# Down product of two FFNs as 2x2 block products of column chunk pairs, with seven products in some k-tile pairs

## Chip, cores and metric

The kernel runs on one core of a Trainium2 chip. The metric is device time in microseconds, the median of several executions; one further execution was recorded by the hardware profiler, and all rows below come from it.

## The reference

One decoder layer on 256 tokens of width 2048 in float32: half an FFN, a token mixer (two head groups of attention that read one input projection), another half FFN. The change touches the two FFNs (d_ff is 5632) and, at its edges, what stands next to them:

```python
def swiglu(x, w_gate, w_up, w_down):
    return (jax.nn.silu(x @ w_gate) * (x @ w_up)) @ w_down

x = x + 0.5 * swiglu(rms_norm(x, ffn1_norm[l]), ffn1_w_gate[l], ffn1_w_up[l], ffn1_w_down[l])
h = rms_norm(x, mix_norm[l])
parts = jnp.split(h @ w_in[l], split_at, axis=-1)
...
x = x + y @ w_out[l]
x = x + 0.5 * swiglu(rms_norm(x, ffn2_norm[l]), ffn2_w_gate[l], ffn2_w_up[l], ffn2_w_down[l])
```

## The kernel before

Tokens are two tiles of 128 (t = 0, 1), contraction goes in k-tiles of 128, columns in chunks of 512. Every product is made of three matmuls: both operands are split into a rounded high part and the rest (`split`, L195: a ScalarE cast to fp32r, a VectorE subtraction), and high x high, low x high and high x low are summed in one PSUM bank. Weights stream from memory into `w_raw` (three buffers), and are split into `w_hi` and `w_lo` (two buffers each).

An FFN goes over its 11 column chunks in parts of 4, 4 and 3 (`FF_PARTS`). For the first chunk gate and up are made as two plain products (`plain_pair`, `linear`); for every other chunk `pair` makes them together. A pair of k-tiles, the two token tiles and the two weight chunks (gate, up) form a 2x2 by 2x2 block product, eight products of three matmuls each. At the k-tile pairs j = 1, 3, 5 of eight (`STRASSEN`) it is made with seven products of sums instead: sums of activation blocks (S1 to S4, NS3) and sums of weight blocks (`w_t`, split into `t_hi`, `t_lo`, one buffer each). At the other j four of the eight products use differences (S3, DD) so that the results fall into the same PSUM sums. These are m2, m4, m5, m3 in the four main banks and m1, m6, m7 in three side banks; the fourth side bank serves all transposes meanwhile (`misc`). Behind the last seven step s1, v and u are formed, at the end seven more VectorE operations and two SiLUs make the chunk's result `g`. Then main and side banks swap (`banks.swap`).

The activation sums of x are made once for an FFN (`put_sums`, from a scaled copy `xf`). A chunk's result is transposed on TensorE in two halves of four transposes (`to_gT`, L358) and split into `ghi` and `glo` by one cast and one subtraction a half. After each part the down product runs over four column chunks, one after the other, with the plain `linear` (L217 on): per k-tile six matmuls, no sums, all four side banks free for transposes. Its result is added to the residual `xr` by two VectorE operations a chunk (L487). In the last part each finished chunk of `xr` goes on at once: in FFN 1 it is normalised for the mixer (`Stage.chunk`: transposes, splits, squares), in FFN 2 it is sent out (`to_out`).

Background work is written as generators (`spawn`); `pump` gives each one step after every six matmuls, and `wait(n)` lets n steps pass. The program order on each engine is set by a scheduler that lays instructions out by modelled times. `fpool` holds the temporaries of an FFN; in FFN 1 it closes in the last part behind the first down chunk (`to_mixer`), and the pool of the mixer's temporaries opens behind FFN 1.

## Time and profile before

| | us |
|---|---|
| median of 3 runs | 1868.89 (1868.73 to 1869.9) |
| profiled execution | 1867.15 |
| its span, first to last instruction | 1865.4 |
| TensorE busy | 1851.4 (99%) |
| VectorE busy | 1307.1 (70%) |
| ScalarE busy | 895.9 (48%) |
| granted TensorE clock, mean | 0.999 |

The three parts of FFN 1 lie at 5 to 729 us, the mixer at 729 to 1150, FFN 2 at 1150 to 1861. Within an FFN stretches of pairs and stretches of down follow each other. Matmuls overlap, so the busy time of one (about 0.39 us) is not what it takes; the distance between starts is.

### The profile page before, as it was taken

The numbers are of one execution on the slowest core, as the hardware profiler recorded it, in microseconds if no ns is written. First come the engines' busy times: TensorE is split into PE (matmuls) and PEld (weight loads), VectorE is DVE, ScalarE is ACT, GpSimd is POOL, SyncE is SP. The second block draws the span as 40 slices with busy tenths as digits, with TensorE's granted clock in tenths as the row PEclk, the third lists the DMA queues.
The fourth block names the chain that finished last, engine by engine and source line by source line (L and its number), as shares of the span: only waits on it lengthen the run. The fifth ranks groups of instructions, "written<-read, shape, count | busy, mean of one in ns | idle before, by whom it ended". The sixth has DMA issues, their size and how long they took to land.

```text
span 1865.4 us, 21669 instructions
## 1 busy us (share of the span) xinstructions
PE 1851.4 (99%) x8624; PEld 1528.4 (82%) x8626; DVE 1307.1 (70%) x1334; ACT 895.9 (48%) x904; POOL 4.8 (0%) x23
## 2 busy tenths in 40 slices
PE   9999999999999999999999999999999999999999
PEld 7778888888888888788888888888888887888887
DVE  6888568887478865656655567788647887558864
ACT  7545435454345445345455555454434554335542
POOL 0000000000000000000000000000000000000000
PEclk9999999999999999999999999999999999999999
DMA  8655555565566556764533445656556555556654
GB/s 298 208 190 186 194 190 202 194 202 191 189 216 203 195 200 203 237 219 147 155 128 113 144 161 192 203 182 201 198 187 208 198 195 188 192 191 204 203 195 143
DMA packets 190565, 356.60 MB, mean 191 GB/s; under 512 B 9312, under 2 KB 26624, under 8 KB 190464
## 3 DMA queue, kind: packets, MB, share of 16 engines
q1 hardware_dynamic: 188720, 354.65, 57.1%
q8 instruction: 67, 1.10, 0.2%
q10 hardware_dynamic: 1744, 0.58, 0.1%
q14 instruction: 34, 0.28, 0.0%
HBM read 353.09 MB, written 2.10 MB: 190 GB/s over the span
## 4 chain that ended last, share of the span: by engine, by line
PE 97%; ACT 1%; DVE 1%; issue 1%; DMA 0%; SPq 0%; ACTq 0%
PE m L449 15%; PE m L451 15%; PE m L450 15%; PE down L258 9%; PE down L259 9%; PE down L260 9%; PE in L260 4%; PE in L258 4%; PE in L259 4%; PE wo L258 1%; PE wo L259 1%; PE wo L260 1%; PE gt L366 1%; PE no L866 1%; PE gate L258 1%; PE gate L259 1%
## 5 line engine op out<-in xcount | busy, mean ns | idle before, releaser
L197 DVE TENSOR_TENSOR w_lo<-w_raw,w_hi 128x2048 fp32r<-128x2048 f32 (+3 forms) x331 | 709.1, 2148 | 365.0 <-ACT w_hi L196 364.5
L196 ACT CAST w_hi<-w_raw 128x2048 fp32r<-128x2048 f32 (+3 forms) x331 | 591.2, 1798 | 628.8 <-PE down L259 242.0
L449 PE MATMUL m<-w_hi,xhi 128*128 128x512 f32 x980 | 384.0, 392 | 2.2 <-ACT w_hi L196 1.9
L450 PE MATMUL m<-w_hi,xlo 128*128 128x512 f32 x980 | 381.9, 390 | 0.0
L451 PE MATMUL m<-w_lo,xhi 128*128 128x512 f32 x980 | 320.1, 390 | 0.8 <-DVE w_lo L197 0.8
L259 PE MATMUL down<-w_hi,glo 128*128 128x512 f32 x704 | 274.3, 390 | 0.0
L258 PE MATMUL down<-w_hi,ghi 128*128 128x512 f32 x704 | 273.2, 390 | 0.0
L260 PE MATMUL down<-w_lo,ghi 128*128 128x512 f32 x704 | 260.9, 390 | 0.0
L449 PEld LDWEIGHTS m<-w_hi,xhi 128*128 128x128 f32 x980 | 184.0, 188 | 43.5 <-ACT w_hi L196 5.3
L451 PEld LDWEIGHTS m<-w_lo,xhi 128*128 128x128 f32 x980 | 183.9, 188 | 41.2 <-DVE w_lo L197 2.9
L450 PEld LDWEIGHTS m<-w_hi,xlo 128*128 128x128 f32 x980 | 184.0, 188 | 37.7
L197 DVE TENSOR_TENSOR t_lo<-w_t,t_hi 128x2048 fp32r<-128x2048 f32 x60 | 137.3, 2288 | 47.2 <-ACT t_hi L196 47.2
L196 ACT CAST t_hi<-w_t 128x2048 fp32r<-128x2048 f32 x60 | 114.6, 1910 | 103.6 <-DVE w_t L435 101.3
L258 PEld LDWEIGHTS down<-w_hi,ghi 128*128 128x128 f32 x704 | 132.2, 188 | 27.3
L259 PEld LDWEIGHTS down<-w_hi,glo 128*128 128x128 f32 x704 | 132.2, 188 | 27.1
L260 PEld LDWEIGHTS down<-w_lo,ghi 128*128 128x128 f32 x704 | 131.9, 188 | 27.1
L258 PE MATMUL in<-w_hi,xhi 128*128 128x512 f32 (+3 forms) x384 | 146.1, 381 | 0.0
L259 PE MATMUL in<-w_hi,xlo 128*128 128x512 f32 (+3 forms) x384 | 143.8, 375 | 0.0
L260 PE MATMUL in<-w_lo,xhi 128*128 128x512 f32 (+3 forms) x384 | 141.2, 379 | 1.0 <-DVE w_lo L197 0.9
L449 PE MATMUL m<-t_hi,xhi 128*128 128x512 f32 x240 | 94.5, 397 | 1.8 <-ACT t_hi L196 1.8
L432 DVE TENSOR_TENSOR w_t<-w_raw 128x1024 f32<-128x1024 f32 x60 | 73.2, 1221 | 29.1 <-DMA w_raw<-in_ffn_w_gate 28.5
L450 PE MATMUL m<-t_hi,xlo 128*128 128x512 f32 x240 | 92.9, 390 | 0.0
(248 smaller groups left out, 1795.2 us busy)
## 6 DMA issues: line engine op xcount, KB each, us to landing
w_raw<-in_ffn_w_down SPq DMA_DIRECT2D x88, 1024.0 KB, 5.0
w_raw<-in_ffn_w_gate SPq DMA_DIRECT2D x163, 512.0 KB, 4.7
w_raw<-in_ffn_w_up SPq DMA_DIRECT2D x160, 512.0 KB, 3.8
w_raw<-in_w_in SPq DMA_DIRECT2D x36, 1024.0 KB, 5.0
w_raw<-in_w_out SPq DMA_DIRECT2D x16, 1024.0 KB, 4.9
w_raw<-in_ffn_w_up SPq DMA_DIRECT2D x8, 1024.0 KB, 5.4
w_raw<-in_ffn_w_gate SPq DMA_DIRECT2D x6, 1024.0 KB, 5.1
w<-in_cmp_k_w SPq DMA_DIRECT2D x8, 512.0 KB, 6.4
```

The costliest lines, as they stand in the source:

```text
L196: cast = nc.scalar.copy(hi, src)
L197: nc.vector.tensor_tensor(lo, src, hi.bitcast(F32), op=ALU.subtract)
L258: nc.tensor.matmul(po[t][:, :n], xhi, whi[:, j], start=s, stop=False)
L259: nc.tensor.matmul(po[t][:, :n], xlo, whi[:, j], start=False, stop=False)
L260: nc.tensor.matmul(po[t][:, :n], xhi, wlo[:, j], start=False, stop=e)
L366: nc.tensor.transpose(pt[:, j * SEQ + t * P:j * SEQ + (t + 1) * P], sg[t][:, (2 * i + j) * P:(2 * i + j + 1) * P], ident)
L432: nc.vector.tensor_tensor(ts[:, 0:2], raw[:, 0:1].to_broadcast([P, 2, CH]), raw[:, 1:4:2], op=ALU.subtract)
L449: nc.tensor.matmul(pm[m], ahi, bhi, start=first, stop=False)
L450: nc.tensor.matmul(pm[m], alo, bhi, start=False, stop=False)
L451: nc.tensor.matmul(pm[m], ahi, blo, start=False, stop=end)
L866: nc.tensor.matmul(po[:, h * HD:(h + 1) * HD], pT[:kn, h * P:(h + 1) * P], vv, start=first and h == 0, stop=True, skip_group_check=True)
```

## The change

`blocks` is `pair`'s loop made general: the weights' loads, the source of the activation forms, the seven steps and an action behind the last of them (`middle`) are arguments. `pair` calls it as before. `down` calls it for two column chunks at a time (0 and 1, then 2 and 3), with the 2x2 blocks of `g` in place of x and the two chunks of w_down in place of gate and up. Seven steps are those of j = 1, 3, 5 that are below nj - 1: three of eight pairs in the parts of four chunks, two of six in the last part. `middle` adds s1, v and u to the residual behind the last seven step; five more additions follow at the end. `to_gT` makes the sums of `g` once per part, for each half from a copy `gf` of the transposes. In the last part the residual chunks are handed on in the middle of the end additions and behind them. Around it: the pools are divided, so that `fpool` with the weight sums stays open until FFN 1's end (`fxpool` holds the forms of x); `xf` shares the buffers of `w_t` and `t_lo`; s1, v, `gf` and the rotary angles share one buffer; the sums of x start 8 instead of 14 pumps behind a load; squares go to PSUM; the two masks become one, read with a zero stride; the start-up zeros use a weight buffer.

```diff
-    idle = spool.tile([P, CH], BF16, tag="sq", bufs=1, name="idle")
+    idle = wpool.tile([P, CH], BF16, tag="wlo", name="idle")
...
-            self.pool = None
+            self.pool = self.tmp = None
         def square(self, c):
             for t in range(NT):
-                sq = spool.tile([P, CH], F32, tag="sq", bufs=1, name="sq")
-                nc.scalar.activation(sq, xr[t][c], AF.Square, accum_out=self.ssq[:, t, c:c + 1])
+                nc.scalar.activation(misc("sq"), xr[t][c], AF.Square, accum_out=self.ssq[:, t, c:c + 1])
...
             yield from wait(later)
             n = self.width(gi)
-            xf = self.pool.tile([P, 8, P], F32, tag="xf", bufs=2, name="xf")
+            xf = self.tmp.tile([P, 8, P], F32, tag=("ts", "tlo")[gi % 2], name="xf")
...
     def ffn(st, wg, wu, wd, after, fpool, last_part, groups=None):
-        ghi, glo = {}, {}
+        g = {}
...
-        def to_gT(slot, sg):
+        wdv = wd.rearrange("(k p) n -> p k n", p=P)
+        def to_gT(slot, sg, odd):
             yield from wait(2)
-            hi = gpool.tile([P, 4, SEQ], F32R, tag=f"ghi{slot}", name="ghi")
-            lo = gpool.tile([P, 4, SEQ], F32R, tag=f"glo{slot}", name="glo")
+            hi = gpool.tile([P, 8, P], F32R, tag=f"ghi{slot}", name="ghi")
+            lo = gpool.tile([P, 8, P], F32R, tag=f"glo{slot}", name="glo")
+            xhi = fpool.tile([P, 5, P], F32R, tag=f"gxhi{slot}", name="gxhi")
+            xlo = fpool.tile([P, 5, P], F32R, tag=f"gxlo{slot}", name="gxlo")
+            def put(x, o, n, src):
+                h, l = ((hi, lo), (xhi, xlo))[x]
+                split(h[:, o:o + n], l[:, o:o + n], src)
+            def where(x, o):
+                h, l = ((hi, lo), (xhi, xlo))[x]
+                return h[:, o], l[:, o]
             for i in range(2):
-                pt = misc("gt")
-                for j in range(2):
-                    for t in range(NT):
-                        nc.tensor.transpose(pt[:, j * SEQ + t * P:j * SEQ + (t + 1) * P],
-                                            sg[t][:, (2 * i + j) * P:(2 * i + j + 1) * P], ident)
-                split(hi[:, 2 * i:2 * i + 2].rearrange("p a b -> p (a b)"),
-                      lo[:, 2 * i:2 * i + 2].rearrange("p a b -> p (a b)"), pt)
+                seven = i == 1 and odd
+                pt = misc("gt").rearrange("p (a b) -> p a b", b=P)
+                order = ((0, 1), (0, 0), (1, 0), (1, 1)) if seven else ((0, 0), (0, 1), (1, 0), (1, 1))
+                for n, (j, t) in enumerate(order):
+                    nc.tensor.transpose(pt[:, n], sg[t][:, (2 * i + j) * P:(2 * i + j + 1) * P], ident)
+                gf = fpool.tile([P, 8, P], F32, tag="sv", name="gf")
+                nc.scalar.copy(gf[:, :4], pt)
+                if seven:
+                    put(1, 0, 3, pt[:, 1:])
+                    nc.vector.tensor_tensor(gf[:, 4], gf[:, 0], gf[:, 1], op=ALU.subtract)
+                    nc.vector.tensor_tensor(gf[:, 5:7], gf[:, 0:5:4], gf[:, 3:4].to_broadcast([P, 2, P]), op=ALU.add)
+                    nc.vector.tensor_tensor(gf[:, 7], gf[:, 2], gf[:, 6], op=ALU.subtract)
+                    put(0, 4, 4, gf[:, 4:])
+                    g[2 * slot + 1] = {A11: where(1, 0), A12: where(1, 1), A22: where(1, 2), NS3: where(0, 4),
+                                       S1: where(0, 5), S2: where(0, 6), S4: where(0, 7)}
+                else:
+                    put(0, 4 * i, 4, pt)
+                    nc.vector.tensor_tensor(gf[:, 4:6], gf[:, 0:3:2], gf[:, 1:4:2], op=ALU.subtract)
+                    o = 0 if i else 3
+                    put(1, o, 2, gf[:, 4:6])
+                    g[2 * slot + i] = {A11: where(0, 4 * i), A21: where(0, 4 * i + 1), A12: where(0, 4 * i + 2),
+                                       A22: where(0, 4 * i + 3), S3: where(1, o), DD: where(1, o + 1)}
                 yield False
-            ghi[slot], glo[slot] = hi, lo
-        def glhs(k, t):
-            while k // 4 not in ghi:
+        def gform(j, f):
+            while j not in g:
                 pump()
-            return ghi[k // 4][:, k % 4, t * P:(t + 1) * P], glo[k // 4][:, k % 4, t * P:(t + 1) * P]
+            return g[j][f]
...
-        def pair(c):
+        def blocks(nj, sevens, form, load, middle):
...
-            cols = slice(c * CH, (c + 1) * CH)
-            nj = KD // 2
...
             for j in range(nj):
-                if j in STRASSEN:
+                if j in sevens:
                     plan.append([(1, A11, 1), (2, A12, 2), (3, S4, 3), (5, S1, 4), (7, NS3, 5), (6, S2, 6), (4, A22, 7)])
...
             for j in range(nj):
                 raw = wpool.tile([P, 4, CH], F32, tag="raw", bufs=3, name="w_raw")
-                nc.sync.dma_start(raw[:, 0:4:3], wuv[:, 2 * j:2 * j + 2, cols])
-                nc.sync.dma_start(raw[:, 1:3], wgv[:, 2 * j:2 * j + 2, cols])
+                newest["load"] = load(j, raw)
...
-                if j in STRASSEN:
-                    split(whi[:, 1:4], wlo[:, 1:4], raw[:, 1:4])
+                if j in sevens:
+                    newest["cast"] = split(whi[:, 1:4], wlo[:, 1:4], raw[:, 1:4])
...
                 else:
-                    split(whi, wlo, raw)
+                    newest["cast"] = split(whi, wlo, raw)
                 for i, (m, f, s) in enumerate(plan[j]):
-                    ahi, alo = st.form(j, f)
+                    ahi, alo = form(j, f)
...
-                if j == max(STRASSEN):
-                    s1, v, u = ev("s1"), ev("v"), ev("u")
+                if j == max(sevens):
+                    sv = fpool.tile([P, 2, CH], F32, tag="sv", name="sv")
+                    s1, v, u = sv[:, 0], sv[:, 1], ev("u")
                     nc.scalar.copy(s1, pm[1])
                     nc.vector.tensor_tensor(v, pm[6], s1, op=ALU.add)
                     nc.vector.tensor_tensor(u, pm[7], v, op=ALU.add)
+                    middle(s1, v, u)
+            return pm, s1, v, u
+        def pair(c):
+            cols = slice(c * CH, (c + 1) * CH)
+            def load(j, raw):
+                nc.sync.dma_start(raw[:, 0:4:3], wuv[:, 2 * j:2 * j + 2, cols])
+                return nc.sync.dma_start(raw[:, 1:3], wgv[:, 2 * j:2 * j + 2, cols]).ins
+            pm, s1, v, u = blocks(KD // 2, STRASSEN, st.form, load, lambda *a: None)
...
+        def down(k0, nj, ca, cb, ready):
+            def load(j, raw):
+                rows = slice(k0 + 2 * j, k0 + 2 * j + 2)
+                nc.sync.dma_start(raw[:, 0:4:3], wdv[:, rows, cb * CH:(cb + 1) * CH])
+                return nc.sync.dma_start(raw[:, 1:3], wdv[:, rows, ca * CH:(ca + 1) * CH]).ins
+            def add(t, c, x):
+                nc.vector.scalar_tensor_tensor(xr[t][c], x, 0.5, xr[t][c], op0=ALU.mult, op1=ALU.add)
+            def middle(s1, v, u):
+                add(0, ca, s1)
+                add(0, cb, v)
+                add(1, ca, u)
+                add(1, cb, u)
+            pm, s1, v, u = blocks(nj, [j for j in STRASSEN if j < nj - 1], gform, load, middle)
+            add(0, ca, pm[2])
+            add(1, ca, pm[4])
+            if ready:
+                ready(ca)
+            add(0, cb, pm[5])
+            add(1, cb, pm[5])
+            add(0, cb, pm[3])
+            banks.swap()
+            if ready:
+                ready(cb)
         for pi, (c0, c1) in enumerate(FF_PARTS):
-            ghi.clear()
-            glo.clear()
+            g.clear()
+            final = pi == len(FF_PARTS) - 1
+            nj = 2 * (c1 - c0)
             for c in range(c0, c1):
                 sg = pair(c) if c else plain_pair(c)
-                spawn(to_gT(c - c0, sg))
-            for c in range(4):
-                pd = linear(wd, c0 * 4, (c1 - c0) * 4, c * CH, CH, glhs, "down")
-                final = pi == len(FF_PARTS) - 1
-                if final and c == 0:
-                    last_part()
-                for t in range(NT):
-                    nc.vector.scalar_tensor_tensor(xr[t][c], pd[t], 0.5, xr[t][c], op0=ALU.mult, op1=ALU.add)
-                if final:
-                    after(c)
-    fctx = ExitStack()
+                i = c - c0
+                spawn(to_gT(i, sg, 2 * i + 1 in STRASSEN and 2 * i + 1 < nj - 1))
+            if final:
+                last_part()
+            for c in (0, 2):
+                down(c0 * 4, nj, c, c + 1, after if final else None)
+    fctx, fxctx = ExitStack(), ExitStack()
     fpool = fctx.enter_context(tc.tile_pool(name="fpool1", bufs=1))
     st1 = Stage(0, True)
-    st1.pool = fpool
+    st1.pool = fxctx.enter_context(tc.tile_pool(name="fxpool1", bufs=1))
+    st1.tmp = fpool
...
-        st1.put(gi, xt, 14)
+        st1.put(gi, xt, 8)
...
-        rot = spool.tile([P, 4, NT, 64], F32, tag="sq", bufs=1, name="rot")
+        rot = fpool.tile([P, 4, NT, 64], F32, tag="sv", name="rot")
...
+    xctx = ExitStack()
     def to_mixer():
-        fctx.close()
-        st2.pool = mctx.enter_context(tc.tile_pool(name="xmpool", bufs=1, reuse_waits="tile"))
+        fxctx.close()
+        st2.pool = xctx.enter_context(tc.tile_pool(name="xmpool", bufs=1, side="right", reuse_waits="tile"))
     ffn(st1, d["ffn1_w_gate"], d["ffn1_w_up"], d["ffn1_w_down"], lambda c: spawn(st2.chunk(c)), fpool, to_mixer,
         [[1, 1, 2], [2, 2], [4], [4]])
+    fctx.close()
...
-                    mk = mask_a.rearrange("p a b -> p (a b)")
+                    mk = mask_k[:, 1:2].to_broadcast([P, 4, P])
                 else:
-                    mk = mask_b.rearrange("p a b c -> p (a b c)")
+                    mk = mask_k[:, None].to_broadcast([P, 2, 2, P])
```

## Rows read from the trace of the kernel before

**Rows 1.** The page, section 1: busy us of each engine, its share, its instructions

```profile
PE 1851.4 (99%) x8624; PEld 1528.4 (82%) x8626; DVE 1307.1 (70%) x1334; ACT 895.9 (48%) x904; POOL 4.8 (0%) x23
```

**Rows 2.** Stretches: length, busy us (count) of PE PEld DVE ACT POOL; clock, DMA

```profile
53.60:186.50 132.90, 129.65 (x575) 104.73 (x574) 112.45 (x125) 67.92 (x54) 0.21 (x1) 1.00 0.58 191
...
445.10:533.10 88.00, 88.00 (x394) 72.95 (x394) 49.80 (x35) 34.03 (x21) 0.00 (x0) 1.00 0.57 192
533.10:659.80 126.70, 126.70 (x566) 104.44 (x565) 104.64 (x86) 62.84 (x44) 0.00 (x0) 1.00 0.61 208
...
728.90:751.50 22.60, 22.59 (x104) 18.33 (x102) 14.10 (x28) 12.13 (x15) 0.00 (x0) 1.00 0.67 229
...
1236.80:1279.20 42.40, 42.40 (x193) 35.06 (x191) 36.40 (x31) 20.35 (x16) 0.00 (x0) 1.00 0.60 198
...
1409.70:1580.30 170.60, 169.81 (x757) 139.45 (x756) 140.61 (x115) 84.97 (x60) 0.00 (x0) 1.00 0.59 197
```

**Rows 3.** Tile down alone in a stretch (PE PEld DVE), then TensorE's timeline

```profile
445.10:533.10 88.00, 87.33 (x384) 71.84 (x384) 4.12 (x6) 1.00 0.57 192
...
1859.21 0.39 PE L258 MATMUL down<-w_hi,ghi 128*128 128x512 f32 x1
1859.44 0.39 PE L259 MATMUL down<-w_hi,glo 128*128 128x512 f32 x1
```

**Rows 4.** TensorE's waits: for whom, us in total, times, the longest

```profile
PE gate L258 <- ACT w_hi L196: 2.2, 1, 2.2
PE m L449 <- ACT w_hi L196: 1.9, 4, 1.3
```

**Rows 5.** VectorE groups by shape: count, busy us, mean ns, idle before

```profile
L197 DVE TENSOR_TENSOR w_lo<-w_raw,w_hi 128x2048 fp32r<-128x2048 f32 x254 | 580.4, 2290 | 347.9 <-ACT w_hi L196 347.5
...
L197 DVE TENSOR_TENSOR w_lo<-w_raw,w_hi 128x1536 fp32r<-128x1536 f32 x64 | 112.0, 1750 | 0.5 <-ACT w_hi L196 0.5
L432 DVE TENSOR_TENSOR w_t<-w_raw 128x1024 f32<-128x1024 f32 x60 | 73.2, 1221 | 29.1 <-DMA w_raw<-in_ffn_w_gate 28.5 <-DVE w_lo L197 0.5
L435 DVE TENSOR_TENSOR w_t<-w_raw,w_t 128x512 f32<-128x512 f32 x60 | 41.3, 688 | 1.1
...
L487 DVE SCALAR_TENSOR_TENSOR xr<-down,xr 128x512 f32<-128x512 f32 x48 | 32.5, 690 | 19.7 <-PE down L260 19.7
L197 DVE TENSOR_TENSOR glo<-gt,ghi 128x512 fp32r<-128x512 f32 x44 | 29.6, 684 | 5.4 <-ACT ghi L196 5.4
...
L317 DVE TENSOR_TENSOR xf<-xf 128x256 f32<-128x256 f32 x10 | 4.2, 424 | 3.2 <-ACT xf L309 3.2
...
L197 DVE TENSOR_TENSOR xlo<-xf,xhi 128x256 fp32r<-128x256 f32 x10 | 4.0, 418 | 0.0
...
L312 DVE TENSOR_TENSOR xf<-xf 128x128 f32<-128x128 f32 x6 | 1.6, 284 | 0.0
```

**Rows 6.** Chain that ended last, FFN 1 first pairs: start, us, what

```profile
71.06 0.68 ACT g L389
72.56 1.92 ACT w_hi L196
```

**Rows 7.** TensorE's timeline in a pair of FFN 2

```profile
1248.74 0.60 PE L366 MATMUL gt<-ident,g 128*128 128x128 f32 x4
...
1254.91 0.60 PE L366 MATMUL gt<-ident,g 128*128 128x128 f32 x4
...
1258.12 1.07 PE L451 MATMUL m<-t_lo,xhi 128*128 128x512 f32 x4
```

**Rows 8.** Timelines at FFN 1's end: VectorE, then TensorE

```profile
675.78 0.28 DVE L598 TENSOR_TENSOR tabC<-cos_t,gb 128x128 f32<-128x128 f32 x1
...
731.59 0.60 PE L326 MATMUL xt<-ident,xr 128*128 128x128 f32 x4
```

**Rows 9.** VectorE's timeline at the end of the kernel

```profile
1860.77 1.37 DVE L487 SCALAR_TENSOR_TENSOR xr<-down,xr 128x512 f32<-128x512 f32 x2 [6.19 <-PE down L260]
```

**Rows 10.** SP's timeline in a pair of FFN 2

```profile
1242.14 0.37 SPq L425 DMA_DIRECT2D w_raw<-in_ffn_w_up  x1
```

17 lines of the change are left out of this document (9 added, 8 removed).

## The prediction

> **What bounds the kernel now.** I read the shares of the page first: TensorE is busy 99% of the span, VectorE 70%, ScalarE 48% [rows 1]. Busy matmuls can hide waits, so next come the stretches cut by stage [rows 2]. The down stretch from 445.1 to 533.1 holds 384 matmuls and 8 transposes; the matmuls alone are busy for 87.33 us, 0.227 each, which is also the distance of their starts [rows 3]. 384 x 0.227 = 87.1, and the 0.9 left are 0.11 for each transpose. Down has no stall at all. A gate/up pair has 183 matmuls (three k-pairs with seven products, five with eight, three matmuls each) and two sets of four transposes: 41.5 + 0.9 = 42.4, and the pair from 1236.8 took 42.40. The three pairs from 533.1 have 549 matmuls and 16 transposes: 126.4 of 126.7, so 0.1 us a pair is lost; the four from 1409.7 have 732 and 24: 168.8 of 170.6, 0.45 a pair. Only FFN 1's first pairs lose more: 549 and 24 make 127.3 of 132.9. All that TensorE waited for is 9.9 us in the list of its waits, eight entries of which the two largest are shown [rows 4]. So the number of matmuls sets the time, and VectorE is the next engine: 36.40 of 42.40 us in a pair, 49.80 of 88.00 in a down [rows 2].
>
> **The change, part by part.**
>
> *Matmuls removed.* A down over two column chunks has per k-pair 8 products of three matmuls; a seven saves one product, three matmuls. Sevens are at j = 1, 3, 5 where j < nj-1: three for nj = 8, but only two (1, 3) for the last part's nj = 6. Per FFN (3+3+2) x 2 column pairs = 16 sevens, 32 in both: 96 matmuls of 0.227 us = **-21.8 us**. They are on the path, since down has no stall that could take their place.
>
> What a matmul is worth can be read in another way. LDWEIGHTS is busy 82% against TensorE's 99% [rows 1]. The Trainium skill, "Perfetto Trace Analysis", section "Identifying the Most-Contended Engine", calls matmul busy time a bad measure and wants MFU and LDWEIGHTS busy share. By that the price would be a weight load's 0.187 us (71.84 over 384 [rows 3]) and the saving 18.0 us. The starts, 0.227 apart with no wait between, speak for the row; I give the other a small chance.
>
> *VectorE work added in down.* A seven step replaces a 2.290 split by one of 1.750, sums of 1.221 and twice 0.688 and another split of 2.290 [rows 5]: 6.64 us against 21 x 0.227 = 4.77 of TensorE, so a seven step alone is VectorE-bound. A plain step is 2.29 against 5.44, and one of each 8.93 against 10.2. That is the pattern the pairs already run with 0.1 to 0.45 us lost. A pair without its transposed splits (2 x 0.684) has 35.0 us of VectorE, nine evictions of 512 columns among it (about 0.69 each); a down block has eleven (v, u, four adds behind the last seven step, five at the end), so 35.0 + 2 x 0.69 = 36.4 of 41.5 us (88%). Before, the two columns had 24.9 of 44.0. Nothing shows where a stall first bites: the bounds are 0 (down before) and 1.9 a block (FFN 1's first pairs, 5.6 over three); I take 0.3, the mean of the steady pairs, which run the same pattern: 12 blocks x 0.3 = **+3.6** (0 to 22.8).
>
> *Activation sums, made when a chunk's transposes are split.* A plain half adds a difference of 256 columns (0.424) and its split (0.418): 0.84 us of VectorE. A seven half adds two sums of 128 columns (0.284), one of 256 (0.424) and a split of 384 columns, about 0.55 (an estimate between the 0.418 of 256 and the 0.684 of 512): 1.54 [rows 5]. Eight of the 22 halves per FFN are seven. In a pair this makes at most 36.4 + 2.4 = 38.8 of 42.4 us (91%), in a part's first down, where the last chunk's two halves are plain, 36.4 + 3.1 = 39.5 of 42.4 (93%), and with nj = 6 (one seven and one plain step less, 8.9) 30.6 of 32.2 (95%). ScalarE gets a copy of 512 columns and a cast of 256 or 384 more per half, about 1.6 us a chunk (an estimate from the 1.92 of a 2048-column cast [rows 6] by columns); it is busy 20.35 of 42.40 [rows 2], so its idle half hides it. But a cast that waits for a VectorE sum holds up the weight cast queued behind it, and through that TensorE. In down the transposes now have one PSUM bank instead of four. In a pair that is so already, and the second set follows 6.2 us after the first [rows 7]; the last chunk's sums are wanted six steps into down, 30 us later (four steps, 20 us, where nj is 6). I take 0.1 for each of the 16 pairs with such a chunk, **+1.6** (0 to 0.6 each, 9.6).
>
> *FFN 1 into the mixer.* Before, three of four columns had been normalised when "in" began, and its last chunk's transposes came 2.7 us into it [rows 8]. Now the second column pair closes together, so chunks 2 and 3 both fall into the first product, chunk 2 wanted at k = 8, 48 x 0.227 = 10.9 us in, and with twice the splits in that time. Chunks 0 and 1 must pass one bank in the last down (four groups and four squares). The rotary tables, twelve operations like that of 0.28 us, lay in down from 675.78 [rows 8]; their pool now opens only after FFN 1, so 3.4 us of VectorE moves into the first 22.6 us of "in", where it is busy 14.1 [rows 2]. It fits, with little room: **+1.5** (0 to 4).
>
> *Opening.* Of the 5.6 us that FFN 1's first pairs lost, most lies at 67 to 76, where the chain runs from a weight cast over the first chunk's SiLU, which waited for the row scale, to the cast queued behind it [rows 6]. The sums of x move six pumps earlier, out of this stretch into the plain pair; the angles share their buffer with the new sums and with s1 and v, and the temporaries of x's sums share that of the weight sums, so each may wait for the other. Both signs are possible: **0** (-4 to +4).
>
> *End.* The last matmul was followed by two additions, 1.37 us, and the output transfers [rows 9]. Now only the last product's addition remains: **-0.7** (-0.7 to 0).
>
> *No cost.* The loads are the same bytes in two transfers of 512 KB instead of one of 1 MB; SP issues one such transfer in 0.37 us [rows 10], and a step of 4.77 us or more has two, so the queue is mostly idle and hides it; if it were not hidden, 88 issues more would be 33 us at most. Out-transfers stand in that queue before later loads, as they did. Squares written to PSUM, one mask read with a zero stride in place of two, the start-up zeros in another buffer: a few operations, off the path, hidden by the same engines' idle time.
>
> Sum: -21.8 + 3.6 + 1.6 + 1.5 + 0 - 0.7 = **-15.8 us**. The profiled execution took 1867.15 us for a span of 1865.4; it becomes 1851.4. The median of the runs shown is 1868.89, 1.7 above it, so I predict **1853.1 us**.
>
> **The rivals.**
>
> *VectorE's additions show (slower).* The place is the seam of two phases: the adds behind the last seven step, the end adds, the transposed sums and the first seven step's sums come within some 20 us, and the weight sums have one buffer each, so a late split is a late matmul. The additions over what pairs carry today are 16 x 2.4 for the pairs, 12 x 1.4 for the blocks, 6 x 3.1 for the first downs, and 3.4 for the tables: 38 + 17 + 19 + 3 = 77 us. From 21.8/77 = 28% on, shown as stalls, the gain is gone. At half it would be +38.5 - 21.8: 1885.6 us. For it: 91 to 95% of a phase is more than any steady phase has now. Against: the matmuls with w_lo and t_lo are already put several places behind those with w_hi (the four of t_lo run in a row at 1258.12 [rows 7]), VectorE is idle for 6 us of every pair, and no phase reaches 100%. 5%; with the price near a quarter the result is no change, another 5%.
>
> *All of it hides.* Down blocks lose nothing, like down before: -21.8 - 0.7: 1846.4. For it: down's stall of zero; against: steady pairs do lose. 18%.
>
> *A matmul is worth its weight load only*, if starts drew together where weights are loaded less often: 96 x 0.187 [rows 3] is -18.0 in place of -21.8: 1856.9. Against it are the even starts 0.227 apart. 5%.
>
> *It does less than it says.* Only two sevens in the last part is in the sum already. If the last part's blocks, the tightest, each paid 1.9 us and the seam its 4: four blocks x 1.6 more + 2.5 = +8.9: 1862.0. 10%.
>
> **How the numbers follow.** The forecast (1848 to 1858) has 57%, the rivals 5 + 5 + 18 + 5 + 10%. The range of 1845.5 to 1862.0 leaves out the two 5% cases and parts of the opening's ends, some 15% in all; its low end is full hiding with 0.9 us of the opening. About 0.2% is what a measurement of this kernel can tell from no change: faster 0.90, the same 0.05, slower 0.05.
>
> **What would show it.** Down's matmuls: 366 per part of eight, 276 for the last, in 83 to 85 and 63 to 66 us. TensorE's list of waits should grow from 10 to about 17 us, with the splits w_lo and t_lo and the casts ahead of them as names; VectorE's share should go to about 84% (1307 + 32 x 4.35 for seven steps + 84 x 0.69 for adds + 48 for sums, over 1849.6). Wrong would be matmul starts further apart than 0.227 in down, a repeated gap at each start of a down or pair, or a gap of several us after "in" begins.

## The result, and the profile after

The changed kernel takes 1920.98 us (median of four runs, 1919.57 to 1922.66) against 1868.81 for the kernel before: a ratio of 1.0278 [1.0260, 1.0296], **slower by 52 us** where 16 us less was predicted. The profiled execution has a span of 1917.9 us against 1865.4. Cut where the same products begin, the 52.5 us lie here (before against after, us):

| stretch | before | after | difference |
|---|---|---|---|
| start, FFN 1's plain pair | 53.6 | 54.9 | +1.3 |
| FFN 1's pairs and down blocks | 675.3 | 705.7 | +30.4 |
| mixer, to its last attention | 321.3 | 323.3 | +2.0 |
| wo, FFN 2's plain pair | 144.2 | 147.3 | +3.1 |
| FFN 2's pairs and down blocks | 667.0 | 682.4 | +15.4 |
| end | 4.0 | 4.3 | +0.3 |

The page of after, section 1 (compare [rows 1]):

```profile
PE 1871.1 (98%) x8530; PEld 1510.1 (79%) x8530; DVE 1517.5 (79%) x1665; ACT 981.2 (51%) x1036; POOL 3.9 (0%) x22
```

TensorE has 94 records less (96 matmuls by the code) and is busy 20 us longer. That points at the matmuls themselves, which the list of waits cannot show. The starts settle it. TensorE in a pair of FFN 2 (start, length, line, operands), whose matmuls the change leaves as they were:

```profile
1241.45 0.39 PE L475 MATMUL m<-t_hi,xlo 128*128 128x512 f32 x1
...
1242.38 0.39 PE L474 MATMUL m<-w_hi,xhi 128*128 128x512 f32 x1
```

Four starts on in 0.93 us, 0.232 each, against 0.227 in [rows 3]. Over the 2838 matmuls of an FFN's pairs and down blocks the difference of 0.005 is an estimated 15 us, about 30 in both. The rest is in stalls. The waits of TensorE (for whom, us in total, times, longest; [rows 4] has the same view) and five stretches (length, busy PE PEld DVE ACT POOL, clock, DMA, as in [rows 2]):

```profile
PE m L474 <- ACT t_hi L194: 9.5, 16, 0.6
PE xt L325 <- ACT sq L280: 8.9, 1, 8.9
PE m L476 <- DVE w_lo L195: 8.2, 7, 2.1
PE m L474 <- ACT sv L483: 6.9, 1, 6.9
```

```profile
54.90:760.60 705.70, 678.23 (x2944) 543.31 (x2943) 606.34 (x601) 354.98 (x286) 0.33 (x2) 0.99 0.58 191
1231.20:1913.60 682.40, 674.03 (x2926) 539.70 (x2925) 587.86 (x543) 344.33 (x270) 0.00 (x0) 1.00 0.57 189
99.00:111.00 12.00, 2.97 (x9) 1.65 (x8) 10.45 (x24) 1.98 (x4) 0.00 (x0) 0.70 0.53 174
112.00:114.00 2.00, 2.00 (x6) 1.61 (x5) 2.00 (x4) 0.85 (x2) 0.00 (x0) 0.50 0.00 0
748.00:760.60 12.60, 3.70 (x20) 2.87 (x18) 10.65 (x24) 5.62 (x8) 0.00 (x0) 0.81 0.75 238
```

Two places stand out, with 9 us of stall each, one at 100 to 110 (2.12 and 6.92 us) and one at the end of FFN 1. The granted clock falls in both: from 112 to 114, behind the first, it is 0.50, which is TensorE's lower level of 1.2 GHz, and the matmuls from 110.69 to 114.10 start 0.427 us apart. They cost 1.9 us more by that, and those behind the second stall about 1 us, part of the mixer's +2.0. All through the FFNs there are short stalls of 0.3 to 1.3 us.

**The stall at 100 to 110.** The timelines of TensorE, ScalarE and VectorE there (idle time before, and what ended it, in brackets):

```profile
102.68 0.49 PE L476 MATMUL m<-w_lo,xhi 128*128 128x512 f32 x1 [2.12 <-DVE w_lo L195]
110.10 0.80 PE L474 MATMUL m<-w_hi,xhi 128*128 128x512 f32 x1 [6.92 <-ACT sv L483]
110.69 0.63 PE L475 MATMUL m<-w_hi,xlo 128*128 128x512 f32 x1
111.12 0.63 PE L476 MATMUL m<-w_lo,xhi 128*128 128x512 f32 x1
```

```profile
98.29 1.48 ACT L194 CAST w_hi<-w_raw 128x1536 fp32r<-128x1536 f32 x1 [0.45 <-ACT t_hi L194]
108.32 0.31 ACT L615 ACTIVATE sin_t<-rot 128x128 f32<-128x128 f32 x1 [8.55 <-DVE rot L614]
109.12 0.31 ACT L619 ACTIVATE cos_t<-rot 128x128 f32<-128x128 f32 x1 [0.48 <-DVE rot L618]
109.46 0.58 ACT L483 COPY sv<-m 128x512 f32<-128x512 f32 x1
```

```profile
97.75 0.68 DVE L195 TENSOR_TENSOR glo<-gf,ghi 128x512 fp32r<-128x512 f32 x1
```

The first pair's copy of its sum m1 (`sv`) follows the rotary angles by 0.03 us: the angles (`rot`) have the buffer that `sv` needs, and their seventeen small operations lie on VectorE between the weights' (the first at 100.55, the last at 108.86). The 2.12 us ahead of it are for a split of weights that VectorE makes from 100.88 on, behind the first of them. The angles in turn begin behind the last use of `gf`, which has the same buffer (VectorE's line at 97.75). In the kernel before, with another buffer, they ran from 59.3 to 70.8. So three tenants stand in a row.

**The stall at the end of FFN 1.** The transposes of FFN 1's result, then VectorE between them:

```profile
748.68 0.60 PE L325 MATMUL xt<-ident,xr 128*128 128x128 f32 x4
759.81 1.12 PE L325 MATMUL xt<-ident,xr 128*128 128x128 f32 x4 [8.90 <-ACT sq L280]
```

```profile
749.55 0.69 DVE L523 SCALAR_TENSOR_TENSOR xr<-m,xr 128x512 f32<-128x512 f32 x1 [1.09 <-PE m L476]
750.16 2.28 DVE L195 TENSOR_TENSOR w_lo<-w_raw,w_hi 128x2048 fp32r<-128x2048 f32 x1
...
754.37 1.28 DVE L523 SCALAR_TENSOR_TENSOR xr<-m,xr 128x512 f32<-128x512 f32 x2
755.57 2.28 DVE L195 TENSOR_TENSOR w_lo<-w_raw,w_hi 128x2048 fp32r<-128x2048 f32 x1
757.76 0.48 DVE L200 SCALAR_TENSOR_TENSOR xlo<-xt,gains,xhi 128x256 fp32r<-128x256 f32 x1
758.16 0.68 DVE L523 SCALAR_TENSOR_TENSOR xr<-m,xr 128x512 f32<-128x512 f32 x1
```

The group of transposes that waits is the fourth of eight, the second one of column chunk 1. Two readings are open. The squares share the transposes' bank and end just ahead of them; and VectorE works without a gap from 750.16 to 758.84, on the last additions, two weight splits, the splits of the transposes and eight operations of the rotary tables.

**A short stall**, in FFN 2 at 1525: TensorE, ScalarE, VectorE.

```profile
1525.21 0.50 PE L474 MATMUL m<-t_hi,xhi 128*128 128x512 f32 x1 [0.60 <-ACT t_hi L194]
1525.55 0.40 PE L475 MATMUL m<-t_hi,xlo 128*128 128x512 f32 x1
...
1526.91 0.39 PE L475 MATMUL m<-t_hi,xlo 128*128 128x512 f32 x1
```

```profile
1521.45 1.91 ACT L194 CAST w_hi<-w_raw 128x2048 fp32r<-128x2048 f32 x1 [6.67 <-PE m L475]
1523.26 1.90 ACT L194 CAST t_hi<-w_t 128x2048 fp32r<-128x2048 f32 x1
```

```profile
1519.19 0.68 DVE L460 TENSOR_TENSOR w_t<-w_raw,w_t 128x512 f32<-128x512 f32 x1
1519.80 0.28 DVE L388 TENSOR_TENSOR gf<-gf 128x128 f32<-128x128 f32 x1
1523.39 2.29 DVE L195 TENSOR_TENSOR w_lo<-w_raw,w_hi 128x2048 fp32r<-128x2048 f32 x1 [3.31 <-ACT w_hi L194]
```

VectorE is idle for 3.31 us just there, so it is not out of time. The sums `w_t` were ready at 1519.9, but ScalarE's queue has the next step's `w_hi` first, which waits for a buffer that TensorE reads, and `t_hi` starts at 1523.26.

### The profile page after: what moved, and what is told of

The parts are those of the page before. It is cut to its first block, busy times and chain, and to the rows that moved or that the text cites. A ratio compares the mean times of both kernels' runs of the same rounds, so it can differ in the third digit from the quotient of the medians.

```text
span 1917.9 us, 22306 instructions
## 1 busy us (share of the span) xinstructions
PE 1871.1 (98%) x8530; PEld 1510.1 (79%) x8530; DVE 1517.5 (79%) x1665; ACT 981.2 (51%) x1036; POOL 3.9 (0%) x22
## 4 chain that ended last, share of the span: by engine, by line
PE 91%; DVE 3%; ACT 3%; DMA 2%; issue 1%; ACTq 0%; SPq 0%; DVEq 0%
PE m L474 22%; PE m L476 22%; PE m L475 22%; PE in L258 4%; PE in L256 4%; PE in L257 4%; DVE w_lo L195 2%; ACT t_hi L194 1%; PE wo L256 1%; PE wo L258 1%; PE wo L257 1%; DMA w_raw<-in_ffn_w_gate 1%; PE gt L380 1%; ACT w_hi L194 1%; PE no L935 1%
## 5 line engine op out<-in xcount | busy, mean ns | idle before, releaser
L195 DVE TENSOR_TENSOR w_lo<-w_raw,w_hi 128x1536 fp32r<-128x1536 f32 (+3 forms) x331 | 691.7, 2096 | 215.2 <-ACT w_hi L194 200.8
L194 ACT CAST w_hi<-w_raw 128x1536 fp32r<-128x1536 f32 (+3 forms) x331 | 574.9, 1755 | 549.8 <-PE m L475 367.1
L195 DVE TENSOR_TENSOR t_lo<-w_t,t_hi 128x2048 fp32r<-128x2048 f32 x92 | 210.4, 2287 | 49.4 <-ACT t_hi L194 49.4
L194 ACT CAST t_hi<-w_t 128x2048 fp32r<-128x2048 f32 x92 | 175.5, 1908 | 74.5 <-DVE w_t L460 73.4
L474 PE MATMUL m<-w_hi,ghi 128*128 128x512 f32 x368 | 145.2, 396 | 0.9 <-ACT w_hi L194 0.7
L475 PE MATMUL m<-w_hi,glo 128*128 128x512 f32 x368 | 145.2, 395 | 0.0
L476 PE MATMUL m<-w_lo,ghi 128*128 128x512 f32 x368 | 131.3, 397 | 3.8 <-DVE w_lo L195 3.8
L476 PEld LDWEIGHTS m<-w_lo,ghi 128*128 128x128 f32 x368 | 69.2, 188 | 22.2 <-DVE w_lo L195 6.1
L474 PEld LDWEIGHTS m<-w_hi,ghi 128*128 128x128 f32 x368 | 69.1, 188 | 18.7 <-ACT w_hi L194 3.3
L256 PEld LDWEIGHTS in<-w_hi,xhi 128*128 128x128 f32 x384 | 72.6, 189 | 13.6 <-issue 3.1
```

The lines of the kernel that those rows point to most:

```text
L194: cast = nc.scalar.copy(hi, src)
L195: nc.vector.tensor_tensor(lo, src, hi.bitcast(F32), op=ALU.subtract)
L256: nc.tensor.matmul(po[t][:, :n], xhi, whi[:, j], start=s, stop=False)
L474: nc.tensor.matmul(pm[m], ahi, bhi, start=first, stop=False)
L475: nc.tensor.matmul(pm[m], alo, bhi, start=False, stop=False)
L476: nc.tensor.matmul(pm[m], ahi, blo, start=False, stop=end)
```

## Experiments

**Where the tiles lie.** The diff has one more line, which neither the section on the change nor the prediction names: three paddings.

```diff
-PAD_C, PAD_S = 256, 320
+PAD_C, PAD_S, PAD_X = 128, 192, 96
```

They move every tile behind them. In the built programs, modulo 512 bytes of a partition, weights, sums of weights, gated tiles and forms of x (the split activations) lie at 0 before. After, weights lie at 384, the others at 256, and the mixer's forms at 384. Theory A: a matmul slows when its moving operand (weights) and its stationary one (forms) differ there. Theory B: the added work of VectorE and ScalarE slows it. Four runs, two of them of the kernel before with a padding changed and nothing else:

```diff
e1_align         (after)   PAD_C, PAD_S, PAD_X = 256, 320, 96
e2_align_all     (after)   PAD_C, PAD_S, PAD_X = 256, 320, 480
e3_before_pads   (before)  PAD_C, PAD_S = 128, 192
e4_before_shift  (before)  PAD_C, PAD_S = 128, 320
```

> The changed kernel with the two paddings of the kernel before (256 and 320 bytes in place of 128 and 192), and nothing else: the weight tiles, the forms of the activations, the sums and their weights all start at multiples of 512 bytes of a partition. Only the mixer's activations (xmpool, laid out from the right end) stay 384 bytes off a multiple of 512, while the weights that meet them no longer are. Theory A (a product is held up when its moving and its stationary operand lie at different offsets modulo 512 bytes): starts inside the FFN stretches go back from about 232 to 227 ns, 2 x 2838 products x 5.2 ns = 30 us, 3 us more in the plain pair and wo, and up to 1152 x 5 ns = 5 us lost in 'in'; 1921 - 33 + 4 = 1892 us. Theory B (VectorE's and ScalarE's added work holds TensorE up at the memory): starts stay at 232 ns, 1921 us.

> As the run before, and the padding behind the mixer's activations is 480 bytes in place of 96, so these too start at multiples of 512. Theory A: all products at 227 ns, 1921 - 33 = 1888 us, and 'in' at 227 ns as in the kernel before. Theory B: 1921 us. If the time equals that of the run before, what counts is the stationary forms' own offset and not that of the pair, or 'in' has no room to lose.

> The kernel before with the paddings of the changed kernel (128 and 192 bytes in place of 256 and 320), and nothing else: weight tiles 384 bytes off a multiple of 512, forms of the activations and the gated tiles 256 off. No engine gets any work more. Theory A: starts in both FFNs go from 227 to about 232 ns, 5868 products x 5.2 = 30 us, 3 us more in the plain pair and wo, up to 5 in 'in': about 1869 + 36 = 1905 us. Theory B: 1869 us, no change.

> The kernel before with the first padding alone at 128 bytes, so that moving and stationary operands both lie 384 bytes off a multiple of 512. Theory A in its form of a difference between the two: no change, 1869 us. Theory A in its form of an offset of its own (only multiples of 512 are quick): about 1905 us, as in the run before. Theory B: 1869 us.

Measured: e1 1896.2 us, ratio to before 1.0149 [1.0134, 1.0164]; e2 1893.9, 1.0137 [1.0122, 1.0153]; e3 **1904.7**, 1.0195 [1.0178, 1.0212]; e4 1869.4, 1.0004 [0.9995, 1.0014]. A down stretch of e3 and of e4, tile down alone, as in [rows 3]:

```profile
455.40:545.60 90.20, 89.53 (x384) 72.06 (x384) 4.15 (x6) 1.00 0.57 187
```

```profile
446.20:534.10 87.90, 87.25 (x384) 71.81 (x383) 4.12 (x6) 1.00 0.57 192
```

384 matmuls in 89.53 us, 0.233 each, and in 87.25, 0.227, as before. In the mixer's `in` of e1, whose forms alone are off:

```profile
799.96 0.40 PE L257 MATMUL in<-w_hi,xlo 128*128 128x512 f32 x1
...
801.13 0.39 PE L257 MATMUL in<-w_hi,xlo 128*128 128x512 f32 x1
```

Five starts on in 1.17 us, 0.234; in e2, with these aligned as well, 0.227. After itself shows it too: right behind the short stall at 1525, six starts with `t_hi`, which lies at 256 like the forms, take 1.36 us, 0.227 each, in a block whose products with `w_hi` and `w_lo` start 0.232 apart. So theory A stands, in the form of a difference: e4, both operands at 384, costs nothing, and e3 costs 36 us with no engine given any work and no wait added (TensorE's longest is 2.4 us, 2.2 before). Theory B does not: down in e3 has VectorE busy for 49.88 of 90.20 us, no more than before. Over the 7404 matmuls of 512 columns in the kernel before the 36 us are 4.8 ns each. Only differences of 0 and of 128 (modulo 512) were tried, and what in the chip makes the difference no run shows.

In the changed kernel the paddings cost 27 us [1893.9 against 1921.0], not the 33 of theory A. TensorE, VectorE and ScalarE have the same order in both; with quicker matmuls the stalls grow, in FFN 2 by 3 to 4 us (it goes from 682.4 to 671.2 us, where the starts are worth 14 to 15). The Trainium skill, "SBUF — State Buffer", section "SBUF: two separate sides", says that on the engines' side only the port pair shared by VectorE and GpSimd causes contention, and that PE never waits on anyone. In e3 the place of TensorE's own two operands changes its time by 36 us, so here the measurement decides.

The following runs change e2_align_all (1893.9 us) further. Its four executions lie between 1890.5 and 1897.5 us, so a run that is 1 to 4 us off is not told from it by its time.

**The angles' buffer.**

```diff
-        rot = fpool.tile([P, 4, NT, 64], F32, tag="sv", name="rot")
+        rot = fpool.tile([P, 4, NT, 64], F32, tag="gxhi3", name="rot")
```

> On the kernel with all operands at multiples of 512 bytes (1893.9 us): the rotary angles' scratch gets a buffer of its own (that of the last slot's forms, free until much later) in place of the buffer tag that it shares with gf and with s1 and v. Theory (the shared buffer makes the first pair's copy of its first sum wait for the angles, and TensorE with it): the two stalls at 98 to 108 us, 2.4 + 7.2 us, are gone; 1893.9 - 9.6 = 1884.3 us. Rival (VectorE is behind there anyway, with the sums of the activations and the first gated tile): the stall stays or moves to the next step, within 3 us of 1893.9.

1882.7 us, 11.2 less: the 9 us of stall and the matmuls at the lower clock behind it. From 99 to 111 TensorE is now busy all along, beside a VectorE that has no pause either. The angles now run from 8.6 to 24.2, so the shared buffer had cost two things, the wait and seventeen operations moved into a full stretch; e5 takes both away together:

```profile
99.00:111.00 12.00, 11.93 (x51) 9.25 (x52) 12.00 (x15) 5.77 (x6) 0.00 (x0) 1.00 0.49 170
```

**The end of FFN 1.** Squares to SBUF; tables later:

```diff
-                nc.scalar.activation(misc("sq"), xr[t][c], AF.Square, ...
+                sq = spool.tile([P, CH], BF16, tag="sq", bufs=1, name="sq")
+                nc.scalar.activation(sq, xr[t][c], AF.Square, ...
```

```diff
-    tabC, tabS = make_tables()
+    with tc.issue_after(newest["cast"].ins):
+        tabC, tabS = make_tables()
```

> On the same aligned kernel: the squares are written to a tile in SBUF again, as in the kernel before, not to a bank of PSUM. Theory 1 (the square in the shared bank holds up the transposes of the next chunk at the end of FFN1): the wait of the transposes, 8.9 us at 737 to 746, falls to about 1; 1885 us. Theory 2 (the last chunk's own additions end only at 745.5, behind weights, tables and other additions on VectorE, and the transposes cannot start before): at most 1 us, 1893 us.

> On the same aligned kernel: the sixteen operations of the rotary tables are issued only behind the last weight cast of the mixer's first product, not at the end of FFN1. Theory 2 of the run before (VectorE's queue at the end of FFN1): the last additions to the residual come about 3 to 4 us sooner and the transposes' wait of 8.9 us shrinks by as much; 1890 us. Theory 1 (the bank): the wait stays, 1894 us.

1892.4 and 1891.9 us: 1.5 and 2.0 less, no more than the spread; the wait itself goes from 8.9 to 7.5 and to 7.3 us. The bank with the squares is not the cause: in e6 the same transposes wait for the split of the transposes before them. Then the transposes were moved: called for later (e10), held behind products of `in` by an issue order (e14), and, in two kernels that also have squares in SBUF and the sevens at 2, 4 and 6 (e12 below, 1875.7 us), with more banks (e16) and with all chunks but the first held (e18).

```diff
-            yield from wait(2)
-            self.group(2 * c)
+            yield from wait(late)
+            with tc.issue_after(newest["mm"].ins):   # e14, e18
+                self.group(2 * c)
...
                     middle(s1, v, u)
+                    banks.free = side                # e16
```

> On the aligned kernel: the transposes of the last chunk of FFN1's result are called for five pumps later (seven in place of two), that is at k-tile 7 of the mixer's first product in place of 2; k-tile 12 is the first that needs them. Theory (TensorE waits 8.9 us at the end of FFN1 since these transposes stand in its queue ahead of products that could run, and the additions that they need end only at 745.5): the wait goes, 1885 us. Rival (the first k-tiles' own forms are late as well, since both chunks of the last block end together and VectorE has their splits, the additions and the weights to do): at most half of it goes, 1890 us.

> On the aligned kernel: as the run with the later transposes, which moved nothing since the planner put them at the same place in TensorE's queue; here the last chunk's transposes are held behind the sixth k-tile's products of the mixer's first product by an issue order. Theory (TensorE waits 9 us at the end of FFN1 for transposes in its queue whose additions end late, while products stand behind them): the wait falls to 1 or 2 us, 1886 us. Rival (the first k-tiles' weights or forms are late as well): 1890 us or more.

> On the kernel aligned and with sevens at 2, 4 and 6 (1875.7 us): squares to SBUF; once a block's sums of seven are out of PSUM, its three banks are free for transposes (four banks in place of one); the transposes of the second finished chunk of FFN1 wait for that, and those of the last two chunks are held behind the mixer's sixth and eighth k-tile. Theory (during FFN1's last block the four groups of transposes of the first two finished chunks pass one bank one after another, each round 8 to 11 us since its splits stand behind the weights' splits on ScalarE and VectorE, and the last of them, ahead of the mixer's products in TensorE's queue, is 11 us late): the wait of 10.9 us goes, 1865 us. Rival (the mixer's first products are late for another reason, their own weights or the additions): 1872 us or more.

> On the aligned kernel with sevens at 2, 4 and 6 (1875.7 us): squares to SBUF, and the transposes of FFN1's finished chunks 1, 2 and 3 are held behind the mixer's first, fifth and eighth k-tiles, where other banks are free; in the run before, chunk 1's two groups still shared one bank with chunk 0's and went through it 9 us apart. Theory (four groups of transposes and their splits pass one bank in turn during FFN1's last block, and the last stands ahead of the mixer's products): only chunk 0's two groups are left in the block, the wait of 8.6 to 10.9 us falls to 2 or 3, about 1867 us. Rival (the mixer's first weights or the additions are late by themselves): the wait moves behind the first products of 'in', 1874 us or more.

e10 1893.6, e14 1892.3, e16 1877.5, e18 1879.5 us: none gains. e10, e14 and e16 told little. Late transposes did move (in e10 the last two groups start 12 and 14 us into `in`, in e2 7 and 9, so e14's text is wrong in saying that e10 moved nothing). But the group that waits is that of an earlier chunk, still in turn in one bank (in e16 the first four groups come at 705.68, 715.70, 724.36 and 733.37). e18 took these out of the way too, and the wait went to the products of `in` themselves:

```profile
731.03 0.80 PE L256 MATMUL in<-w_hi,xhi 128*128 128x512 f32 x1 [5.17 <-DVE xr L526]
```

```profile
725.69 1.29 DVE L526 SCALAR_TENSOR_TENSOR xr<-u,xr 128x512 f32<-128x512 f32 x2
726.89 1.29 DVE L526 SCALAR_TENSOR_TENSOR xr<-m,xr 128x512 f32<-128x512 f32 x2
728.09 2.29 DVE L195 TENSOR_TENSOR w_lo<-w_raw,w_hi 128x2048 fp32r<-128x2048 f32 x1
730.29 0.69 DVE L526 SCALAR_TENSOR_TENSOR xr<-m,xr 128x512 f32<-128x512 f32 x1
```

The second accumulator of `in` has the bank of the last block's product, which VectorE reads only at 730.29, 5 us after that block's end. So e18's rival holds: the closing additions are late by themselves, behind each other and a weight split. With sevens at 2 and 4 the middle additions come closer to the end than in the changed kernel, but there too the last addition, shown above, ends at 758.84, 8 us after the block. What of that is amount and what is the order that the planner sets on VectorE stays open; no run put the additions ahead of the split.

**The short stalls.** Amount of VectorE's work, or order? First the order of ScalarE's casts held (e9), the gated tile's sums later (e8, and e13 behind the last seven):

```diff
-                    newest["cast"] = split(whi, wlo, raw)
+                    with tc.issue_after(newest["form"].ins):   # e9: behind t_hi
+                        newest["cast"] = split(whi, wlo, raw)
...
-            yield from wait(2)
+            yield from wait(9)                                 # e8; 22 in e13, gf in w_t's buffer
```

> On the aligned kernel (1893.9 us): the cast of the weights of a step with eight products is issued only behind the cast of the step before's sums of weights (t_hi); no work is added or taken. In the aligned kernel ScalarE's queue has the next step's w_hi ahead of this step's t_hi, w_hi waits for a buffer that TensorE still reads, and TensorE has the next step's first products ahead of this step's t_hi products. Theory (the stalls of 0.35 + 0.78 us at a block's last step with seven products come from this order, not from VectorE's amount of work): the some 20 of them are gone in each FFN; 12 us in FFN2, about as much in FFN1, 1870 us. Rival (VectorE has too much to do in a block): t_lo and w_lo come late in place of t_hi, and the time stays within 5 us of 1894.

> On the same aligned kernel: the transposes, sums and forms of a gated tile are made at the third k-tile pair of the next block in place of the first (they wait for nine pumps in place of two), with the same work on each engine. Theory (the stalls of about 0.35 + 0.8 us, or 1.3, at the second k-tile pair of nearly each block come from VectorE being late there, the gated tile's sums on top of the additions that close a block and of the first weights' sums): some 15 of these in each FFN shrink to about a third, together 15 to 20 us; 1876 us. Rival (VectorE is short of time over the whole block, so that work moved is only late elsewhere): 1894 us, stalls at another pair of k-tiles.

> On the aligned kernel with the order of the casts held (1897.6 us): the gated tile's transposes, sums and forms are made behind the last step with seven products, at the seventh k-tile pair of the next block (22 pumps in place of two), where VectorE has room, with gf in the buffer of w_t. Theory (VectorE's work ahead of the third seven is too much): the t_hi stalls of 1.2 us in the pairs go, those of 2.2 us in the down blocks shrink; FFN2 loses about 10 us of its 18 us of idle time, 1880 us. Rival (order): no change, 1897 us.

e9 1897.6 us, 3.7 more, which is inside the spread. The short waits of 0.2 us for `w_hi` are gone, and those for `t_hi` come to 18.9 us, the longest 2.0, in place of 9.7 and 0.6. VectorE, ScalarE and TensorE in e9:

```profile
1547.74 0.28 DVE L386 TENSOR_TENSOR gf<-gf 128x128 f32<-128x128 f32 x1
1547.95 0.55 DVE L195 TENSOR_TENSOR gxlo<-gt,gxhi 128x384 fp32r<-128x384 f32 x1
1548.41 0.68 DVE L459 TENSOR_TENSOR w_t<-w_raw,w_t 128x512 f32<-128x512 f32 x1
1549.01 0.42 DVE L387 TENSOR_TENSOR gf<-gf 128x256 f32<-128x256 f32 x1
1549.35 0.68 DVE L460 TENSOR_TENSOR w_t<-w_raw,w_t 128x512 f32<-128x512 f32 x1
```

```profile
1550.14 1.90 ACT L194 CAST t_hi<-w_t 128x2048 fp32r<-128x2048 f32 x1 [5.61 <-DVE w_t L460]
```

```profile
1552.10 0.50 PE L475 MATMUL m<-t_hi,xhi 128*128 128x512 f32 x1 [1.05 <-ACT t_hi L194]
```

Now the chain w_t, t_hi, matmul is direct, and three operations of the gated tile's sums, 0.28 + 0.55 + 0.42 = 1.25 us, stand in VectorE's queue among the sums of the weights: about what TensorE loses there. e8 asked for them later and got 1893.1 us, no change. It tested nothing: the planner put them at the same place again (L386 at 1498.41, ahead of a stall of 0.60 at 1505.72, as in after at 1517.59 and 1525.21), and VectorE's order differs from e2's in one block alone. e13, 1973.8 us, tells nothing of its theory: `gf` in the buffer of `w_t` made the next sums wait, 54 us of t_hi waits.

Then the steps of seven at other places:

```diff
-STRASSEN = (1, 3, 5)
+STRASSEN = (2, 4, 6)
```

> On the aligned kernel (1893.9 us): the k-tile pairs with seven products are 2, 4 and 6 in place of 1, 3 and 5, in the pairs and in the down blocks; the number of products and each engine's work are the same. Theory (over the first six steps of a block VectorE has more work than TensorE, with the additions that close the block before, the gated tile's sums and three steps of seven, each 6.7 us of VectorE against 4.8 of TensorE, so that it is 1 to 2 us late at the third): two plain steps ahead of the first seven give it time to catch up, the stalls go or halve; 1875 to 1885 us. Rival (the order that the planner sets is the cause by itself): 1894 us or any shift, with t_hi waits as before.

**1875.7 us**, 18.2 less, the best of all, still 1.0037 [1.0024, 1.0049] of before. The angles' stall is gone as well, so some 11 of the 18 us are the same as in e5: the angles begin at 82.6 there (100.55 in after), and the `sv` copy right behind them, at 94.79, is in time. FFN 2 alone, without such a stall, goes from 671.2 to 665.5 us:

```profile
1203.10:1868.60 665.50, 659.61 (x2927) 539.20 (x2925) 589.17 (x543) 347.74 (x271) 0.00 (x0) 1.00 0.58 193
```

It has the same matmuls and the same work of VectorE (589 us; 588 in after). So the total amount is not what counts. Whether the place of the sevens acts by the order in the queues or by how much work meets in a short stretch, as this run's own theory has it, e12 cannot tell. That theory's 1875 to 1885 us was met by luck: it named the short stalls alone, and of the 15.1 us that FFN 2 idles longer in e2 than in the kernel before (671.2 - 667.0 + 10.9) 9.4 are left, where they were to go or halve. Last, the amount itself: GpSimd makes the gated tile's sums and their low halves (e17, against e16).

```diff
-                    nc.vector.tensor_tensor(gf[:, 4:6], gf[:, 0:3:2], gf[:, 1:4:2], op=ALU.subtract)
+                    nc.gpsimd.tensor_tensor(gf[:, 4:6], gf[:, 0:3:2], gf[:, 1:4:2], op=ALU.subtract)
```

> As the run before, and GpSimd, idle in the FFNs, makes the sums of the gated tiles' parts and the low halves of these sums, some 25 us of VectorE's work in each FFN. Theory (VectorE's amount of work, 94% of the FFN stretches, costs the remaining 9 to 12 us of idle TensorE in each FFN): most of it goes, 5 to 8 us in each FFN less than the run before, 1852 us. Rival (order and latency, not amount): no change against the run before; if GpSimd slows VectorE's operations beside it, slower.

1883.0 us, 5.5 more than e16. Groups of FFN 2 in e17, then one of e16:

```profile
L398 POOL TENSOR_TENSOR gf<-gf 128x256 f32<-128x256 f32 x14 | 25.0, 1787 | 765.3 <-ACT gf L386 765.3
L195 DVE TENSOR_TENSOR w_lo<-w_raw,w_hi 128x1536 fp32r<-128x1536 f32 x46 | 86.4, 1877 | 0.0
```

```profile
L195 DVE TENSOR_TENSOR w_lo<-w_raw,w_hi 128x1536 fp32r<-128x1536 f32 x46 | 80.5, 1750 | 0.0
```

The sum takes about 1.79 us on GpSimd (0.42 on VectorE), and VectorE's splits of 1536 columns go from 1.75 to 1.88 on average; those of 2048 columns stay at 2.29. TensorE's waits for `t_hi` grow from 3.6 to 14.8 us. So e17 doesn't decide amount against order; the work moved is slower and slows a part of the rest.

**All together.** Angles, squares, tables, order and later transposes (e11); the same with the sevens at 2, 4 and 6 and the transposes held (e15).

> All of it together on the aligned kernel: own buffer for the angles (-11), squares to SBUF and the tables later (-1.5, -2), the order of the casts, and the last chunk's transposes later. If the parts add up: 1894 - 11 - 12 - 12 - 8 = 1851 us, which is the sum of the prediction (1853) and quicker than the kernel before. If VectorE sets the pace once the stalls are gone: about 1870 us.

> All together on the aligned kernel: own buffer for the angles, squares to SBUF, tables later, casts' order held, sevens at 2, 4 and 6, last chunk's transposes held. If the parts add up: 1894 - 11 - 8 - 20 to 25 = 1850 to 1855 us, quicker than the kernel before and the sum of the prediction. If VectorE is short over whole blocks: 1870 us or more.

1888.2 and 1883.7 us. e15's sum counts the angles' stall twice, by e5 and inside e12. Even so e15 has all that e12 has and takes 8 us more. TensorE's waits for `t_hi`, in e12 and in e15:

```profile
PE m L474 <- ACT t_hi L194: 4.3, 10, 0.6
```

```profile
PE m L478 <- ACT t_hi L194: 19.3, 18, 2.0
```

They are 18.9 us in e9 and 23.6 in e11, which hold the order of the casts too, and 9.7 in e2, which does not. So that order is the likely cost; e15 without it was not run. No version of the changed kernel beats the kernel before.

## Why the prediction was wrong

The forecast missed by 67.9 us (1921.0 against 1853.1). Two steps failed. The first took the price of all other matmuls as fixed and the paddings at nothing: 27 us. The second is the overlap: the added work on VectorE and ScalarE and the shared buffers were to hide but for 6.7 us (3.6 + 1.6 + 1.5 + 0), and the stalls came to some 38. The first alone does not explain the result: with the paddings set right (e2) the kernel is still 25 us slower than before.

*Matmuls removed, -21.8.* The number is right, and the price too where operands are aligned (0.227 in e2, where starts did not draw together as the rival of the weight load asked). But "-21.8 us ... on the path" took the price of the other matmuls, about 7300 of 512 columns, as fixed. The paddings changed it: about +30 us by the starts, 27 by e2, 36 by e3 alone on the kernel before. **This is the first step that failed**: the paddings stand in no line of the sum, not even among "No cost". "Matmul starts further apart than 0.227" was named as what would make the prediction wrong, and that came, in pairs too, whose matmuls the change leaves alone.

**The second step that failed** is what was to hide, in the three terms that follow.

*Opening, 0 (-4 to +4).* Both signs came true. The old stall at 67 to 76 is gone: the first pair of FFN 1 takes 43.4 us against 46.5, though its starts are dearer, a gain of 4. The shared buffer was named as a possible wait, and that was the mechanism; its size was wrong: 11.2 us by e5, which makes +7 in all. The bound came from the old stall, a row of another cause. The wait should have been sized by the tenants in a row: `gf`, then the whole life of the angles, seventeen small operations that VectorE does between its weight operations, 8.3 us from 100.55 to 108.86, then `sv`.

*FFN 1 into the mixer, +1.5 (0 to 4).* 8.9 us in after, and still 8.4 in e16. The prediction named that chunks 0 and 1 must pass one bank, and it is their fourth group that waits, but it gave this no price. The sum counted VectorE's work against the length of the first product of `in`, "it fits, with little room". It left out when the work can begin: the five closing additions of the last block and two weight splits come first, and `in` needs the banks that these additions empty (e18).

*VectorE in down, +3.6, and activation sums, +1.6.* Together 5.2. After has 8.4 us in FFN 1 and 11.3 in FFN 2 that neither the starts nor the two large stalls explain (30.4 + 10.9 for 48 matmuls - 15 - 9.0 - 8.9, and 15.4 + 10.9 - 15; the 15 is the estimate above). Of FFN 1's 8.4, 1.9 are the lower clock behind the angles' stall, and the gain of 4 in its first pair is taken off in it, so the short stalls there are about 10. Together some 21 in place of 5, inside the bounds of 0 to 32 but four times the value taken. VectorE came to 79% of a longer span, not 84. Its share was not what counted: it was idle at the stall of 1525, and e12 changes 5.7 us in FFN 2 with the same work. In the two places looked at (1525 in after, 1552 in e9) a sum or a cast that is a few operations late in a queue, with one buffer each for w_t and t_hi, shows on TensorE at once. The rival "VectorE's additions show" named the one buffer of the weight sums and the seams where phases meet, and its quarter of 77 us is about this size; it would have given no change, with a chance of 5%. By e12 the total of the work does not set the price; whether its crowding at the seams does, or the order there, is open.

*Squares to PSUM, no cost.* Near enough: e6 is 1.5 us less, inside the spread.

*End, -0.7.* 4.3 us after the last stretch, against 4.0 before: no gain.

What stays open: 9 us of idle TensorE in FFN 2 of e12 against the kernel before (665.5 - 667.0 + 10.9), 6 in FFN 1 beside the wait at its end (681.0 - 675.3 + 10.9 - 10.7), order or crowding as their cause, and the split of the 9 us ahead of the mixer into amount and order.

## What to carry to other kernels

A change that moves buffers can change the price of every matmul that reads them: compare the distance of starts in a stretch whose code is unchanged before looking at waits, and try the old kernel with the new layout alone. When a step is given a shared buffer, price the wait by the whole life of the other tenants, on the busiest engine that touches them. An engine with room on average can still be late at a seam, so look at what its queue holds there. Before single gains are added, see whether they remove the same stall: 11 of e12's 18 us are those of e5. Where a planner sets the order, look in the trace whether an edit moved anything; e8 did not.

## What the runs showed of the hardware

Back-to-back matmuls of 512 columns start 0.227 us apart where weights and forms lie at the same offset modulo 512 bytes (0 and 0, 256 and 256, or 384 and 384), and 0.232 to 0.234 apart where they differ by 128, with nothing else changed (e3, e4): 36 us of 1869. Behind a stall of 9 us the granted clock was 0.50, and eight starts came 0.427 us apart before it rose again (after, 110.69 to 114.10). GpSimd's tensor_tensor of 256 columns took about 1.25 and 1.79 us in two places of e17 (GpSimd's spans are rough) against VectorE's 0.42, and VectorE's splits of 1536 columns there took 7% longer on average (1750 to 1877 ns), those of 2048 columns no longer (2286 and 2285).
